# First layer of a hybrid decoder trunk: its weight splits on VectorE, its input normalised ahead of the projection, and a shorter build of the S5 power tables

## The chip, the cores and the metric

One core of one Trainium2 chip runs the whole kernel. The metric is device time in microseconds (us), the median of three runs. One further execution was profiled; rows of it are shown below.

## The reference

Two layers of a decoder trunk run on 512 tokens of width 1024, in float32. Each layer computes

```
h = RMSNorm(x) * g_pre
p = h @ W_in                      # columns shared out among 4 mixers
m = concat[GLA, DiffAttn, S5, RG-LRU](p) @ W_out
x = x + RMSNorm(m) * g_post
x = x + RMSNorm(sqrelu(RMSNorm(x) @ W1) @ W2)
```

The S5 mixer is a complex diagonal recurrence and needs tables of powers of its poles, for 128 steps, as cosine and sine parts.

## The kernel before

**Split products.** Each float32 product is made of three products of a faster format. A weight W is split into `wh` (a rounded copy) and `wl = W - wh`; an activation likewise into `h` and `l`. `w_part` does the split of one weight tile: `act.copy` on ScalarE writes `wh` (line 253), and a subtraction on VectorE or on GpSimd writes `wl` (line 254). `E.split_eng`, a string of `g` (GpSimd) and `v` (VectorE) that is cycled by the number of the tile, says which. In layer 1 it is `g` during the projection and the mixers, `gggv` for the output projection, `v` in the feed-forward part. In layer 2 the projection's weights come already split from DRAM (`early_gen` did it during layer 1's feed-forward part), the output projection's too, and the feed-forward part has `gggv`.

**Order.** Each engine runs its own instructions in the order that the scheduler wrote. SyncE issues all loads. Weights are loaded into three `raw` buffers and split into four `wh`/`wl` pairs ahead of their use (`w_get`, `w_split`, `w_load`); `home` can put a split weight into buffers of another pool.

**Layer 1's input.** The program loads `xT`, the input transposed by the host, in eight tiles. `hl` scales each by the gain column and splits it at once (lines 478 and 479). The norm isn't known yet: `SumSq` squares each tile on ScalarE (line 524), adds them up on VectorE (line 530), and TensorE sums over the partitions; VectorE then takes the reciprocal root, `rtok`, and TensorE spreads it to `rbc`, one value for each token. Every result of the projection is multiplied by it when it leaves PSUM (lines 1327, 1340, 1360 and 1374). The first projection, `dqk`, is done by `gemm_first`, which starts with the first tile that is there. 38 products of zeros run on TensorE first (`WARM`).

**Layer 2's input.** It is normalised first, in token-major tiles `X[b, c]`: ScalarE squares and sums (`accum_out`), `root` makes the reciprocal root of one block of 128 tokens (an activation with Sqrt and four VectorE operations), `dg` is the identity matrix times that root, and `make` multiplies X by `dg` on TensorE, which transposes and scales it (line 1298); the result leaves PSUM as `h` (ScalarE, line 1302) and `l` (VectorE, line 1303). `gemm_blocks` runs `dqk` over the first 256 tokens, calls `make(2)` for the others, then runs over these.

**Around them.** In layer 1 the order of the projections is dqk, dv, glr, gqk, gv, gog, u, rg, rx; the mixers' generators run in between (`advance`), and each starts when its inputs are there. `s5_prep_gen(0)` builds S5's tables during layer 1's mixers; `s5_prep_gen(1)` runs during layer 1's feed-forward part. Its powers are made by doubling: for e = 0 to 6, the first 2^e columns give the next 2^e through `cmul`, six VectorE operations (lines 671 to 676), separately for each half h of the states. `rope` reads q and k out of PSUM (line 1040). `diff_gen` runs the differential attention: row maxima (1072), `nb` (1073), exponentials on ScalarE, weights `cc` (1093).

Of the kernel before, what the change touches and what calls it, by code (L numbers as in the profile page):

```python
# [17 lines left out]
P = 128  # L18
# [94 lines left out]
def host_pack(I):  # L113
# [31 lines left out]
    return dict(xT=np.ascontiguousarray(I["x"][0].T), xt=np.ascontiguousarray(I["x"][0]),  # L145
# [25 lines left out]
def hybrid_trunk(ctx, tc, I, out, consts):  # L171
# [11 lines left out]
    def nm(s):  # L183
        uid[0] += 1
        return f"{s}_{uid[0]}"
# [144 lines left out]
    def gemm_first(wids, xs, consume):  # L330

        ps = [(pd if m // 2 % 2 else pg)() for m in range(4)]
        for kh in range(2):
            W = [w_get(w[kh]) for w in wids]

            def prod(m, k):
                cs = slice(m % 2 * P, m % 2 * P + P)
                Wm, kk = W[m // 2], 4 * kh + k
                mm3(ps[m], Wm[0][:, k, cs], Wm[1][:, k, cs], xs[kk][0], xs[kk][1], kk == 0, kk == 7)

            for k in range(2 if kh else 4):
                for m in range(4):
                    prod(m, k)
                yield
            if kh:
                for m in range(4):
                    for k in (2, 3):
                        prod(m, k)
                    with tc.high_priority(offset=O.evp):
                        consume(m, ps[m])  # L350
                    yield

# [159 lines left out]

    class SumSq:

        def __init__(self, eng, tail):
            self.acc, self.eng, self.tail = None, eng, tail
            self.ends = {}

        def add(self, c, src, hf=None):
            if hf is None:
                sq = wq("sq")
                act.activation(sq, src, AF.Square)
                if c >= self.tail:
                    self.ends[c] = sq
                elif self.acc is None:
                    self.acc = sq
                else:
                    self.eng.tensor_tensor(self.acc, self.acc, sq, ALU.add)  # L530
            else:
                if c not in self.ends:
                    self.ends[c] = wq("sq")
                act.activation(self.ends[c][:, 256 * hf:256 * hf + 256], src, AF.Square)

        def tok(self, bs=range(4)):
            ps = psm()
            tl = [self.acc] + list(self.ends.values())
            for b in bs:
                for i, t in enumerate(tl):  # L540
                    pe.matmul(ps[:, b:b + 1], t[:, b * P:b * P + P], C[:, C_BO + 6:C_BO + 7],
                              start=i == 0, stop=i == len(tl) - 1)
            return ps[:, bs[0]:bs[-1] + 1]

    def bcast_tok(col, n=4):
        ps = psm()
        for b in range(n):
            pe.matmul(ps[:, b * P:b * P + P], col[:, b:b + 1].to_broadcast([P, P]), ident,
                      start=True, stop=True)
        return ps[:, 0:n * P]  # L550
# [57 lines left out]
    def s5_prep_gen(l):  # L608
# [580 lines left out]
    sync.dma_start(PV, I["cols"])  # L1189
# [22 lines left out]
    setup_exp()  # L1212
# [28 lines left out]
    def post_norm(grow, g2=None):  # L1241
# [3 lines left out]
        ss, sx, part = small(8, "ss"), small(8, "sx"), small(4, "part")  # L1245
        gB = [wq("gB") for _ in range(2)]
        for c in range(2):
            sync.dma_start(gB[c], grow[:, c * 512:c * 512 + 512].to_broadcast([P, 512]))

            pool.tensor_scalar(gB[c], gB[c], 32.0, None, ALU.mult)  # L1250
        F, dg = {}, {}

        def stat(b, ct, o, f=None):
            act.activation(wq("sq"), o, AF.Square, accum_out=ss[:, 4 * ct + b:4 * ct + b + 1])
            F[b, ct] = o if f is None else f
            v.tensor_tensor(F[b, ct], o, gB[ct], ALU.mult)
            if ct == 0 and b == 3:
                v.tensor_scalar(part, ss[:, 0:4], D * EPS, None, ALU.add)

        def root(a, b):  # L1260

            y, t, xh = (small(1, k) for k in ("qy", "qt", "qh"))
            act.activation(t, a, AF.Sqrt, bias=b)
            v.tensor_scalar(xh, a, b, -0.5, ALU.add, ALU.mult)
            v.reciprocal(y, t)
            v.scalar_tensor_tensor(t, y, xh, y, ALU.mult, ALU.mult)
            v.scalar_tensor_tensor(y, t, 1.5, y, ALU.add, ALU.mult)
            return y

        def finish(b):  # L1270
            sc = root(ss[:, 4 + b:5 + b], part[:, b:b + 1])
            for c in range(2):
                if g2 is None:
                    o = wp.tile([P, 4, 256], F32, tag="raw", name=nm("o"), bufs=NRAW)
                    o = o.rearrange("p k c -> p (k c)")[:, 0:512]
                    v.scalar_tensor_tensor(o, F[b, c], sc, X[b, c], ALU.mult, ALU.add)
                    sync.dma_start(out[0, b * P:b * P + P, 512 * c:512 * c + 512], o)
                else:
                    v.scalar_tensor_tensor(X[b, c], F[b, c], sc, X[b, c], ALU.mult, ALU.add)
                    act.activation(wq("sq"), X[b, c], AF.Square, accum_out=sx[:, 2 * b + c:2 * b + c + 1])  # L1280
            if g2 is None:
                return
# [5 lines left out]
        def make(b):  # L1288
# [16 lines left out]
            for e in range(2):  # L1305
                for c in range(2):
                    spill(b + e, c)
# [3 lines left out]
    for l in range(NL):  # L1311

        O.__dict__.update(LAYER[l])
        if l == 0:
            E.split_eng = O.mix
        E.mix = {}
        st = {}

        rbc = None
        if l == 0:  # L1320
            rbc = cp.tile([P, T], F32, name="rbc")
            act.copy(rbc, bcast_tok(rtok))
        st["cosr"], st["sinr"] = wb("cosr"), wb("sinr")
        for k, c0 in (("cosr", C_COS), ("sinr", C_SIN)):
            sync.dma_start(st[k], consts[:, c0:c0 + T])
            if l == 0:
                v.tensor_tensor(st[k], st[k], rbc, ALU.mult)

        def ev_mul(key):
# [3 lines left out]
            def f(m, ps):  # L1333
                t = w(key)
                o, i, r = t, ps, rbc
                if key == "u":
                    o = t.rearrange("p (s t) -> p s t", s=4)
                    i, r = (x if x is None else x.rearrange("p (t s) -> p s t", s=4) for x in (ps, rbc))
                if l == 0:
                    v.tensor_tensor(o, i, r, ALU.mult)  # L1340
                else:
                    act.copy(o, i)
# [10 lines left out]
        def ev_silu(key):  # L1353
            st[key] = [None, None]

            def f(m, ps):
                t = wg(key)
                if l == 0:
                    v.tensor_tensor(t, ps, rbc, ALU.mult)
                act.activation(t, t if l == 0 else ps, AF.Silu)  # L1360
# [3 lines left out]
        def ev_tok(key):  # L1364
# [4 lines left out]
            def f(b, n, ps):  # L1369
                if l > 0:  # L1370
                    act.copy(tl[b // 2], ps)
                    return
# [185 lines left out]
```

## Time and profile before

| what | value |
|---|---|
| median of 3 runs | 1248.59 us (1243.89 to 1249.86) |
| the profiled execution's own time | 1246.94 us |
| its span, first to last instruction | 1244.9 us |
| TensorE busy | 1201.6 us (97%) |
| VectorE (DVE) busy | 683.9 us (55%) |
| ScalarE (ACT) busy | 509.2 us (41%) |
| GpSimd (POOL) busy | 194.2 us (16%) |
| mean granted TensorE clock | 0.976 |

Busy is time with at least one instruction under way; shares are averages over stages that differ. The chain is the work that ended last, followed back from the end, so that only what lies on it set the time. PE is TensorE, PEld its weight loads, DVE is VectorE, ACT ScalarE, POOL GpSimd, SP SyncE. The names with an arrow are output and input of an instruction, L is the line.

### The profile page before, as it was taken

The numbers are of one execution on the slowest core, as the hardware profiler recorded it, in microseconds if no ns is written. First come the engines' busy times: TensorE is split into PE (matmuls) and PEld (weight loads), VectorE is DVE, ScalarE is ACT, GpSimd is POOL, SyncE is SP. The second block draws the span as 40 slices with busy tenths as digits, with TensorE's granted clock in tenths as the row PEclk, the third lists the DMA queues.
The fourth block names the chain that finished last, engine by engine and source line by source line (L and its number), as shares of the span: only waits on it lengthen the run. The fifth ranks groups of instructions, "written<-read, shape, count | busy, mean of one in ns | idle before, by whom it ended". The sixth has DMA issues, their size and how long they took to land.

```text
span 1244.9 us, 17841 instructions
## 1 busy us (share of the span) xinstructions
PE 1201.6 (97%) x6684; PEld 967.6 (78%) x6684; DVE 683.9 (55%) x1605; ACT 509.2 (41%) x950; POOL 194.2 (16%) x148
## 2 busy tenths in 40 slices
PE   8988899899999999999999999999999999999997
PEld 6755566579888888888889776777988888888886
DVE  8987568578725576545474256575641131322335
ACT  5253622456735523424341356145542341332332
POOL 5321212300000001000000000010123323333330
PEclk9998889999999999999999999899999999999999
DMA  7343122456867887866754432355432333333221
GB/s 229 98 141 116 35 86 82 136 168 208 265 211 235 283 292 241 267 210 212 253 195 141 155 109 91 116 198 203 170 100 88 100 102 92 100 97 101 87 83 67
DMA packets 126037, 191.81 MB, mean 154 GB/s; under 512 B 10688, under 2 KB 65792, under 8 KB 125952
## 3 DMA queue, kind: packets, MB, share of 16 engines
q1 hardware_dynamic: 125952, 190.69, 47.4%
q8 instruction: 52, 0.85, 0.3%
q14 instruction: 33, 0.27, 0.1%
HBM read 146.35 MB, written 44.30 MB: 153 GB/s over the span
## 4 chain that ended last, share of the span: by engine, by line
PE 83%; DVE 10%; ACT 3%; DMA 1%; issue 1%; SPq 0%; DVEq 0%; ACTq 0%
PE pg L295 7%; PE pg L296 7%; PE pg L297 7%; PE pd L296 5%; PE pd L297 5%; PE pd L295 5%; PE pd L415 4%; PE pd L417 4%; PE pd L416 4%; PE pg L415 4%; PE pg L417 3%; PE pg L416 3%; PE pd L1063 2%; PE pm L415 2%; PE pm L416 2%; PE pm L417 2%
## 5 line engine op out<-in xcount | busy, mean ns | idle before, releaser
L253 ACT CAST wh<-raw 128x1024 fp32r<-128x1024 f32 (+1 forms) x160 | 157.4, 985 | 257.4 <-PE pg L416 88.2
L254 POOL TENSOR_TENSOR wl<-raw,wh 128x1024 fp32r<-128x1024 f32 (+1 forms) x69 | 156.9, 2275 | 383.3 <-ACT wh L253 380.7
L295 PE MATMUL pg<-h,wh 128*128 128x512 f32 (+1 forms) x496 | 189.4, 383 | 2.6 <-DVE glr L1392 2.5
L297 PE MATMUL pg<-h,wl 128*128 128x512 f32 (+1 forms) x496 | 188.9, 382 | 0.2 <-DVE wl L254 0.2
L296 PE MATMUL pg<-l,wh 128*128 128x512 f32 (+1 forms) x496 | 188.4, 381 | 0.5 <-DVE l L479 0.5
L254 DVE TENSOR_TENSOR wl<-raw,wh 128x1024 fp32r<-128x1024 f32 (+1 forms) x91 | 105.9, 1164 | 144.2 <-ACT wh L253 144.0
L297 PE MATMUL pd<-h,wl 128*128 128x512 f32 (+1 forms) x336 | 120.7, 360 | 0.0
L295 PE MATMUL pd<-h,wh 128*128 128x512 f32 (+1 forms) x336 | 120.6, 360 | 0.0
L296 PE MATMUL pd<-l,wh 128*128 128x512 f32 (+1 forms) x336 | 120.4, 359 | 0.0
L295 PEld LDWEIGHTS pg<-h,wh 128*128 128x128 f32 x496 | 95.7, 193 | 21.7 <-DVE glr L1392 2.9
L297 PEld LDWEIGHTS pg<-h,wl 128*128 128x128 f32 x496 | 95.7, 193 | 17.6 <-issue 1.4
L296 PEld LDWEIGHTS pg<-l,wh 128*128 128x128 f32 x496 | 95.8, 193 | 17.0 <-DVE l L479 1.2
L1474 DVE TENSOR_TENSOR s<-r 128x512 f32<-128x512 f32 x64 | 56.7, 886 | 87.4 <-ACT r L1473 87.4
L415 PE MATMUL pd<-wh,h 128*128 128x512 f32 x240 | 93.7, 390 | 0.9 <-DMA wh<-early 0.9
L417 PE MATMUL pd<-wl,h 128*128 128x512 f32 x240 | 93.6, 390 | 0.4 <-DVE wl L254 0.4
L416 PE MATMUL pd<-wh,l 128*128 128x512 f32 x240 | 93.4, 389 | 0.0
L415 PE MATMUL pg<-wh,h 128*128 128x512 f32 x208 | 81.4, 391 | 1.4 <-ACT h L475 1.4
L416 PE MATMUL pg<-wh,l 128*128 128x512 f32 x208 | 81.0, 389 | 0.0
L417 PE MATMUL pg<-wl,h 128*128 128x512 f32 x208 | 81.0, 389 | 0.0
L297 PEld LDWEIGHTS pd<-h,wl 128*128 128x128 f32 x336 | 63.6, 189 | 9.4
L295 PEld LDWEIGHTS pd<-h,wh 128*128 128x128 f32 x336 | 63.2, 189 | 9.6 <-ACT wh L253 0.3
L296 PEld LDWEIGHTS pd<-l,wh 128*128 128x128 f32 x336 | 63.5, 189 | 9.4
(421 smaller groups left out, 2162.6 us busy)
## 6 DMA issues: line engine op xcount, KB each, us to landing
raw<-in_ffn_w SPq DMA_DIRECT2D x128, 512.0 KB, 3.9
early<-eh SPq DMA_DIRECT2D x52, 256.0 KB, 3.1
early<-el SPq DMA_DIRECT2D x52, 256.0 KB, 4.1
wh<-early SPq DMA_DIRECT2D x23, 512.0 KB, 3.6
wl<-early SPq DMA_DIRECT2D x23, 512.0 KB, 4.7
ex<-in_w_in SPq DMA_DIRECT2D x36, 256.0 KB, 4.8
raw<-in_w_in SPq DMA_DIRECT2D x14, 512.0 KB, 3.7
xd<-xr SPq DMA_DIRECT2D x24, 256.0 KB, 2.9
```

The lines of the kernel that those rows point to most:

```text
L253: act.copy(h[:, k], raws[i][:, k])
L254: eng.tensor_tensor(lo[:, k], raws[i][:, k], h[:, k].bitcast(F32), ALU.subtract)
L295: pe.matmul(ps, wh, xh, start=first, stop=False, **kw)
L296: pe.matmul(ps, wh, xl, start=False, stop=False, **kw)
L297: pe.matmul(ps, wl, xh, start=False, stop=last, **kw)
L415: pe.matmul(o, xs[kk][0][:, ts_], h, start=kk == 0, stop=False)
L416: pe.matmul(o, xs[kk][1][:, ts_], h, start=False, stop=False)
L417: pe.matmul(o, xs[kk][0][:, ts_], lo, start=False, stop=kk == 7)
L1063: pe.matmul(pp[c], qs[h // 2][r:r + 32, i * P:i * P + P], ks[h // 2][r:r + 32, 0:pp[c].shape[1]], start=i == blocks[0], stop=False, tile_p ...
L1474: v.tensor_tensor(s, r, r, ALU.mult)
```

## The change

- **Splits.** All splits of layer 1 go to VectorE: `mix` and `out` become `v`. Layer 2 keeps `gggv`. The first three weights go to buffers of other pools through `home`.
- **Input.** `xT`, `SumSq`, `bcast_tok`, `gemm_first`, `rtok` and `rbc` are gone. The part of `post_norm` that normalised layer 2's input becomes `pre_norm` (`half`, `done`, `make`), and layer 1 uses it too: token-major x is loaded in the order blocks 0, constants, 1, parameter columns, weights 0 and 1, blocks 2 and 3, weight 2; then `make(0)`, and `gemm_blocks` calls `make(2)`. Results leave PSUM by `act.copy` without a factor. `WARM` is 80.
- **S5.** The first 16 powers of both halves and both parts are made in one tile `pw`, with four VectorE operations for each of four doublings; two ScalarE copies for each half put them into the tables, and only e = 4 to 6 are done for each half.

```diff
+        pw = wq("pw")[:, 0:256].rearrange("p (c j m) -> p c j m", c=2, j=8)
+        pool.memset(pw[:, 0, :, 0:1], 1.0)
+        pool.memset(pw[:, 1, :, 0:1], 0.0)
+
+        def bc2(x, m):
+            return x.unsqueeze(1).unsqueeze(3).to_broadcast([P, 2, 8, m])
+
+        for e in range(4):
+            m = 1 << e
+            wr, wi = (w[:, 8 * e + 8:8 * e + 16] for w in (csw, snw))
+            xa, xb = (wq("cm")[:, 0:16 * m].rearrange("p (c j m) -> p c j m", c=2, j=8) for _ in range(2))
+            tt(xa, pw[:, :, :, 0:m], bc2(wr, m), ALU.mult)
+            tt(xb, pw[:, :, :, 0:m], bc2(wi, m), ALU.mult)
+            tt(pw[:, 0, :, m:2 * m], xa[:, 0], xb[:, 1], ALU.subtract)
+            tt(pw[:, 1, :, m:2 * m], xa[:, 1], xb[:, 0], ALU.add)
+            yield
         for h in range(2):
             js = slice(4 * h, 4 * h + 4)
             tabs = [wt(k) for k in ("COS", "SIN", "RC")]
             ct, st, rc = (t.rearrange("p (j c) -> p j c", j=4) for t in tabs)
-            pool.memset(ct[:, :, 0:1], 1.0)
-            pool.memset(st[:, :, 0:1], 0.0)
-            for e in range(7):
+            for c, t in enumerate((ct, st)):
+                act.copy(t[:, :, 0:16], pw[:, c, js])
+            for e in range(4, 7):
                 m = 1 << e
                 wr, wi = (w[:, 8 * e + 8:8 * e + 16] for w in (csw, snw))
-                cmul(ct[:, :, m:2 * m], st[:, :, m:2 * m], ct[:, :, 0:m], st[:, :, 0:m],
-                     bc(wr, m, js), bc(wi, m, js), 4, m)
+                a_r, a_i = (pw[:, c, js] for c in range(2)) if e == 4 else (ct[:, :, 0:m], st[:, :, 0:m])
+                cmul(ct[:, :, m:2 * m], st[:, :, m:2 * m], a_r, a_i, bc(wr, m, js), bc(wi, m, js), 4, m)
                 yield
...
-    ssq = SumSq(v, 7)
-    xin = []
-    for c in range(8):
-        w2 = (c // 4 * 2, c // 4 * 2 + 1)
-        if c % 4 == 0:
-            for i in w2:
-                w_raw(i)
-                w_open(i)
-        xin.append(wl("x"))
-        sync.dma_start(xin[c], I["xT"][c * P:c * P + P, :])
-        for i in w2:
-            sync.dma_start(raws[i][:, c % 4], specs[i][:, c % 4])
-        XG[c] = hl(xin[c], pv("ln_mix_pre", 0, 8, c))
-        for i, e in zip(w2, (v, pool)):
-            w_part(i, slice(c % 4, c % 4 + 1), e)
-        if c % 4 == 3:
-            for i in w2:
-                del raws[i]
-    pos[:] = [4, 4]
-    sync.dma_start(C, consts[:, 0:C_N])
-    w_load(3 + NRAW)
-    for c in range(8):
-        ssq.add(c, xin[c])
-    ms = small(4, "ms4")
-    v.tensor_scalar(ms, ssq.tok(), 1.0 / D, EPS, ALU.mult, ALU.add)
-    rtok = small(4, "rkeep")
-    v.tensor_copy(rtok, rsqrt(ms, 4))
...
+    def pre_norm(g2, keep):
+        sx, dg = small(8, "sx"), {}
+        def half(b, c):
+            act.activation(wq("sq"), X[b, c], AF.Square, accum_out=sx[:, 2 * b + c:2 * b + c + 1])
+        def done(b):
...
+    E.split_eng = "v"
+    half, done, make = pre_norm(lambda c: pv("ln_mix_pre", 0, 8, c), False)
+    x_load(0)
+    sync.dma_start(C, consts[:, 0:C_N])
+    x_load(1)
+    sync.dma_start(PV, I["cols"])
+    home.update(enumerate((wg, wg, wb)))
+    w_load(1)
+    x_load(2)
+    x_load(3)
+    w_load(2)
+    for b in range(4):
+        for c in range(2):
+            half(b, c)
+        done(b)
+        if b == 1:
+            make(0)
+            setup_exp()
...
-            rbc = cp.tile([P, T], F32, name="rbc")
-            act.copy(rbc, bcast_tok(rtok))
...
-                if l == 0:
-                    v.tensor_tensor(o, i, r, ALU.mult)
-                else:
-                    act.copy(o, i)
+                    o, i = t.rearrange("p (s t) -> p s t", s=4), ps.rearrange("p (t s) -> p s t", s=4)
...
-                g = gemm_first if l == 0 else lambda *a: gemm_blocks(*a, make)
-                g = g(WID[l, "dqk"], XG, lambda m, ps: evs[m // 2](m % 2, ps))
+                g = gemm_blocks(WID[l, "dqk"], XG, lambda m, ps: evs[m // 2](m % 2, ps), make)
...
-WARM = 38
+WARM = 80
...
-         mix='g', out='gggv', ff='v', m_outer=False, on_pool=(), pin=False, wt_act=False, add=(), prep_at=1),
+         mix='v', out='v', ff='v', m_outer=False, on_pool=(), pin=False, wt_act=False, add=(), prep_at=1),
```

## Rows read from the trace of the kernel before

**Rows 1.** The page: the chain that ended last, by engine.

```profile
PE 83%; DVE 10%; ACT 3%; DMA 1%; issue 1%; SPq 0%; DVEq 0%; ACTq 0%
```

**Rows 2.** Windows: us, busy (count) by engine, clock, DMA share, GB/s.

```profile
0.00:10.00 10.00, 8.97 (x58) 7.12 (x58) 6.49 (x28) 7.05 (x15) 4.32 (x10) 1.00 0.79 243
0.00:52.00 52.00, 47.26 (x274) 38.80 (x274) 48.49 (x174) 24.66 (x46) 25.05 (x26) 0.97 0.58 177
52.00:117.00 65.00, 52.36 (x332) 37.77 (x331) 58.71 (x272) 28.09 (x85) 15.04 (x19) 0.90 0.43 138
117.00:227.00 110.00, 100.76 (x794) 69.33 (x793) 71.76 (x166) 42.35 (x77) 23.92 (x20) 0.89 0.24 72
643.00:700.00 57.00, 57.00 (x421) 53.20 (x420) 24.02 (x59) 13.54 (x34) 1.10 (x3) 1.00 0.55 191
700.00:846.00 146.00, 143.73 (x1063) 102.17 (x1061) 85.49 (x230) 69.17 (x165) 7.37 (x13) 0.96 0.39 134
```

**Rows 3.** The chain over 0 to 282 us: start, us, what.

```profile
25.07 2.24 DVE sf L585
...
125.55 2.56 DVE nb L1073
...
228.59 2.77 DVE xc L861
```

**Rows 4.** Single lines, 0 to 282 us: count, ns min/median/max.

```profile
L585 DVE SCALAR_TENSOR_TENSOR sf<-sf,sf x7: 149/155/2330, 23.8 to 27.4; 128x4 f32<-128x4 f32 x7
...
L1073 DVE TENSOR_SCALAR nb<-mx x16: 150/160/2548, 62.6 to 159.6; 128x2 f32<-128x2 f32 x16
...
L861 DVE SCALAR_TENSOR_TENSOR xc<-rx,PV,xc x6: 726/739/2853, 228.5 to 237.6; 128x511 f32<-128x511 f32 x2, 128x510 f32<-128x510 f32 x2, 128x509 f32<-128x509 f32 x2
```

**Rows 5.** GpSimd in order of time, 0 to 320 us.

```profile
125.20 2.40 POOL L254 TENSOR_TENSOR wl<-raw,wh 128x1024 fp32r<-128x1024 f32 x1 [18.54 <-ACT wh L253]
```

**Rows 6.** Line 254, the splits, 0 to 282 us, and its waits.

```profile
L254 POOL TENSOR_TENSOR wl<-raw,wh x27: 740/2382/4332, 6.2 to 245.0; 128x1024 fp32r<-128x1024 f32 x19, 128x256 fp32r<-128x256 f32 x8
L254 DVEq EVENT_SEMAPHORE  x12: 21/21/1309, 5.3 to 278.9; - x12
L254 DVE TENSOR_TENSOR wl<-raw,wh x12: 407/680/1226, 5.4 to 280.5; 128x256 fp32r<-128x256 f32 x8, 128x1024 fp32r<-128x1024 f32 x4
...
  ACT wh L253: 127.5, 24
```

**Rows 7.** Line 1340: the projection's results times the reciprocal norm.

```profile
L1340 DVE TENSOR_TENSOR gqk<-pg,rbc x2: 675/680/684, 72.6 to 81.8; 128x512 f32<-128x512 f32 x2
L1340 DVE TENSOR_TENSOR u<-pg,rbc x2: 1093/1105/1117, 160.4 to 163.9; 128x512 f32<-128x512 f32 x2
```

**Rows 8.** Line 673 by form, 80 to 111 us: busy us, mean ns.

```profile
L673 DVE TENSOR_TENSOR COS<-cm,cm 128x128 f32<-128x128 f32 x2 | 0.6, 286 | 0.0
...
L673 DVE TENSOR_TENSOR COS<-cm,cm 128x4 f32<-128x4 f32 x2 | 0.3, 155 | 0.0
```

**Rows 9.** The first product of each layer, in order of time.

```profile
5.11 0.74 PE L295 MATMUL pg<-h,wh 128*128 128x512 f32 x2
...
647.82 0.28 PE L295 MATMUL pd<-h,wh 128*128 128x256 f32 x1
```

**Rows 10.** Rope's last reads of the first projection, both layers.

```profile
L1040 DVE STREAM_SHUFFLE sh<-pd x2: 759/760/762, 36.5 to 37.8; 128x512 f32<-128x512 f32 x2
...
L1040 DVE STREAM_SHUFFLE sh<-pg x2: 737/739/741, 671.7 to 674.6; 128x512 f32<-128x512 f32 x2
```

**Rows 11.** Normalisation: its products on TensorE, and layer 2's evictions.

```profile
L1298 PE MATMUL pg<-dg,xr x16: 270/275/377, 282.2 to 285.3; 128*128 128x128 f32 x16
...
L1298 PE MATMUL pg<-dg,xr x32: 270/275/275, 642.9 to 880.8; 128*128 128x128 f32 x32
...
L1302 ACT ACTIVATE h<-pm,PV x8: 466/470/474, 647.7 to 659.7; 128x256 fp32r<-128x256 f32 x8
...
L1303 DVE SCALAR_TENSOR_TENSOR l<-pm,PV,h x8: 472/476/485, 648.2 to 660.2; 128x256 fp32r<-128x256 f32 x8
```

More of the change, by code (lines that the diff above doesn't have):

```diff
@@ L144, in host_pack @@
         tab[l, :, K_GLR:K_GLR + P] = I["w_in"][l, :, 512:528].reshape(8, P, 16).transpose(1, 0, 2).reshape(P, P)
-    return dict(xT=np.ascontiguousarray(I["x"][0].T), xt=np.ascontiguousarray(I["x"][0]),
+    return dict(xt=np.ascontiguousarray(I["x"][0]),
                 mpost=np.ascontiguousarray(I["ln_mix_post"]), cols=cols, tab=tab)
@@ L328, in gemm_T @@
                     yield
[L330 to L351, printed above, removed]
     def gemm_blocks(wids, xs, consume, need):
@@ L511, in rsqrt @@
         return y
[L513 to L528, printed above, removed]
-                else:
[L530 to L550, printed above, removed]
     cmask = cp.tile([P, P], BF16, name="cmask")
@@ L1231, in hybrid_trunk @@
-    pos[:] = [4, 4]
-    sync.dma_start(C, consts[:, 0:C_N])
-    w_load(3 + NRAW)
-    for c in range(8):
-        ssq.add(c, xin[c])
-    ms = small(4, "ms4")
-    v.tensor_scalar(ms, ssq.tok(), 1.0 / D, EPS, ALU.mult, ALU.add)
-    rtok = small(4, "rkeep")
-    v.tensor_copy(rtok, rsqrt(ms, 4))
[L1241 to L1282, printed above, removed]
@@ new lines, in root @@
+    def root(a, b):
+        y, t, xh = (small(1, k) for k in ("qy", "qt", "qh"))
+        act.activation(t, a, AF.Sqrt, bias=b)
+        v.tensor_scalar(xh, a, b, -0.5, ALU.add, ALU.mult)
+        v.reciprocal(y, t)
+        v.scalar_tensor_tensor(t, y, xh, y, ALU.mult, ALU.mult)
+        v.scalar_tensor_tensor(y, t, 1.5, y, ALU.add, ALU.mult)
+        return y
+    def pre_norm(g2, keep):
[3 more added lines that the diff above has]
+        def done(b):
@@ L1304, in make, with x_load @@
                                            ALU.mult, ALU.subtract)
-            for e in range(2):
-                for c in range(2):
-                    spill(b + e, c)
+            if keep:
+                for e in range(2):
+                    for c in range(2):
+                        spill(b + e, c)
+        return half, done, make
+    def x_load(b):
+        for c in range(2):
+            X[b, c] = wl("x")
+            sync.dma_start(X[b, c], XD[b, c])
+    E.split_eng = "v"
+    half, done, make = pre_norm(lambda c: pv("ln_mix_pre", 0, 8, c), False)
@@ new lines, in hybrid_trunk, with post_norm, stat, finish @@
+    x_load(0)
[8 more added lines that the diff above has]
+    for b in range(4):
+        for c in range(2):
+            half(b, c)
[3 more added lines that the diff above has]
+            setup_exp()
+    def post_norm(grow, g2=None):
+        ss, part = small(8, "ss"), small(4, "part")
+        half, done, make = pre_norm(g2, True) if g2 is not None else (None, None, None)
+        gB = [wq("gB") for _ in range(2)]
+        for c in range(2):
+            sync.dma_start(gB[c], grow[:, c * 512:c * 512 + 512].to_broadcast([P, 512]))
+            pool.tensor_scalar(gB[c], gB[c], 32.0, None, ALU.mult)
+        F = {}
+        def stat(b, ct, o, f=None):
+            act.activation(wq("sq"), o, AF.Square, accum_out=ss[:, 4 * ct + b:4 * ct + b + 1])
+            F[b, ct] = o if f is None else f
+            v.tensor_tensor(F[b, ct], o, gB[ct], ALU.mult)
+            if ct == 0 and b == 3:
+                v.tensor_scalar(part, ss[:, 0:4], D * EPS, None, ALU.add)
+        def finish(b):
+            sc = root(ss[:, 4 + b:5 + b], part[:, b:b + 1])
+            for c in range(2):
+                if g2 is None:
+                    o = wp.tile([P, 4, 256], F32, tag="raw", name=nm("o"), bufs=NRAW)
+                    o = o.rearrange("p k c -> p (k c)")[:, 0:512]
+                    v.scalar_tensor_tensor(o, F[b, c], sc, X[b, c], ALU.mult, ALU.add)
+                    sync.dma_start(out[0, b * P:b * P + P, 512 * c:512 * c + 512], o)
+                else:
+                    v.scalar_tensor_tensor(X[b, c], F[b, c], sc, X[b, c], ALU.mult, ALU.add)
+                    half(b, c)
+            if g2 is not None:
+                done(b)
@@ L1334, in f @@
                 t = w(key)
[L1335 removed]
+                o, i = t, ps
                 if key == "u":
[L1337 to L1342 removed]
+                    o, i = t.rearrange("p (s t) -> p s t", s=4), ps.rearrange("p (t s) -> p s t", s=4)
+                act.copy(o, i)
                 st[key][m] = t
@@ L1369, in f @@
             def f(b, n, ps):
-                if l > 0:
-                    act.copy(tl[b // 2], ps)
-                    return
-                for i in range(n):
-                    act.activation(st[key][b + i], ps[:, 256 * i:256 * i + 256], AF.Copy,
-                                   scale=rtok[:, b + i:b + i + 1])
+                act.copy(tl[b // 2], ps)
             return f
@@ L1390, in glr_gen @@
             t = wg("glr")[0:32]
-            if l == 0:
-                v.tensor_tensor(t, ps, rbc[0:32], ALU.mult)
-            else:
-                v.tensor_copy(t, ps)
+            v.tensor_copy(t, ps)
             st["glr"] = t
```

11 lines of the change are left out of this document (1 added, 10 removed).

## The prediction

> **What bounds the kernel now.** I read the page's chain first. TensorE holds most of it and VectorE 10% [rows 1], which is at most 124 us of the 1244.9 us span. Then I cut the span into stages with the windows. Layer 1's projection and mixers, up to the normalisation behind the output projection (TensorE's products for it begin at 282.2 us [rows 11]), fill 0 to 282 us. Up to 117 us VectorE is busy 107 of 117 us while TensorE has gaps and runs below its full 2.4 GHz level for part of the time (granted clock 0.90); from 117 to 227 us the clock is 0.89 and neither engine is full [rows 2]. Layer 2 does the same projection and mixers, without weight splits and without building tables: TensorE is busy 57.0 of 57 and 143.7 of 146 us, at 1.00 and 0.96, with VectorE at about half [rows 2]. So the stage that the change touches is late by VectorE, and nearly all of VectorE's 124 us must lie there: they are 0.44 of these 282 us.
>
> The chain in order of time shows what VectorE does there. Between 25 and 229 us it holds 13 pieces of VectorE work of 1.67 to 2.77 us, 29.55 us in all, of which the first, one from the middle and the last are shown [rows 3]. They are no large operations: line 1073 works on two columns and takes 160 ns in the median, but 2548 ns once; line 585 takes 155 ns and once 2330; line 861 739 and once 2853 [rows 4]. GpSimd's row gives the reason: a split runs on GpSimd from 125.20 us for 2.40 us, and the slow line 1073 starts at 125.55 and ends as that split ends [rows 5, 3]. The 27 splits on GpSimd [rows 6] thus stop VectorE, small operation or not.
>
> The Trainium skill says so too: "SBUF — State Buffer", section "SBUF: two separate sides", describes a port pair shared by VectorE and GpSimd that whichever starts first keeps for its whole instruction. The trace agrees, by the 2548 ns beside the 160.
>
> **The change, part by part.** *Stalls.* Without splits on GpSimd the 13 pieces shrink to their ordinary lengths. Those are some 0.16 us for eight, 0.2 to 0.3 for four and 0.74 for line 861 [rows 4, 8], 3.0 us together, so 26.5 us leave the chain. What is late next is TensorE or ScalarE, which were only covered by the stall, so the gain lies between 0 and 26.5. I take two thirds, 17.7, as layer 2 shows TensorE running nearly through where VectorE isn't late [rows 2].
>
> *Splits on VectorE.* 19 whole splits and 8 quarters move from GpSimd. VectorE's whole ones take at most 1.23 us, quarters from 0.41 [rows 6]. At 1.2 us: 19 x 1.2 = 22.8; the first four weights, whole or in two halves, 4.8 in place of some 4 us for 8 quarters on VectorE. Together +23.6 us of VectorE.
>
> *Multiplications by the reciprocal norm.* Ten of 0.68 us go (gqk, rg, rx, gog, and the two rope tables, counted like gqk), two for u of 1.1 and one for glr, counted 0.6: 9.6 us; the six additions of squares, of the same shape, 6 x 0.68 = 4.1; the reciprocal root, some 14 tiny operations, 2.2 [rows 7, 4]. In their place come four roots with `dg`, 4 x 5 tiny operations at 0.16 and 4 x 0.28 (like a form of 128 columns), 4.3 us, and 16 evictions of `l` at 0.476 us for 8 of 512 columns, some +1.5 [rows 4, 8, 11]. ScalarE takes over the copies and sums its squares while squaring them, eight as before; I cost this at nothing, since it is busy 28 of 65 and 42 of 110 us [rows 2]. Without that room the eight or so copies at 0.6 us would be 5 us.
>
> *S5's powers.* Forty-eight operations go (4 to 32 columns), at some 0.17 us each, 8.2 us; 16 with 16 to 128 columns come, at some 0.21, 3.4 (0.155 is measured at 4 columns, 0.286 at 128 [rows 8]): -4.8 us. The four ScalarE copies hide as above. In layer 1's feed-forward part the same saving is hidden by TensorE and worth nothing.
>
> VectorE's own work so changes by 23.6 - 9.6 - 4.1 - 2.2 + 4.3 + 1.5 - 4.8 = +8.7 us. At its share of the chain, 0.44, that costs 3.8 us (0 if it fills gaps, 8.7 if all lies on the path).
>
> *The start.* Before, TensorE's first product is at 5.11 us [rows 9] and `rope` reads the last piece of dqk at 37.8 [rows 10]. Now nothing starts before blocks 0 and 1 of x are there, squared, rooted, transposed and evicted. Bytes: 1.05 MB of x, 0.22 of constants, 0.09 of columns, 1.05 of weights 0 and 1, 2.4 MB; at 243 GB/s [rows 2] 9.9 us, and some 2 us until the first lands: 12; with a cast and a subtraction the first product is at about 13 us. Layer 2's `gemm_blocks` goes from 647.8 to `rope`'s last read at 674.6 [rows 9, 10], 27 us with `make(2)` inside. So dqk ends near 40 us, 2 to 3 us later, and 6 later if weight 3, which waits for one of three raw buffers, is late for the second half. SyncE has fewer loads to issue than before, the two tables of rope need no factor any more, and the longer warm-up ends before the first product, so these cost nothing; without the wait for x the warm-up would be in the way. I take +3 (0 to +6).
>
> *The clock.* From 52 to 227 us it stood at 0.90 and 0.89; layer 2's like stretch has 0.96 [rows 2]. Reaching that would give 65 x 0.06 + 110 x 0.07 = 11.6 us; an estimate of half, 5.8, since VectorE stays fuller than in layer 2.
>
> Sum: -17.7 + 3.8 + 3 - 5.8 = -16.7 us. The profiled execution took 1246.94 us, so 1230.2; the median of the runs is 1.65 above it, so 1232 us. The stages after 282 us stay: TensorE sets them, and layer 2's splits still go to GpSimd.
>
> **The rivals.** *The pace of layer 2* (chance 0.18). If VectorE is never late any more, dqk starts at 13 us and takes what layer 2's part takes: from 647.8 us to the end of the same products, 880.8 [rows 9, 11], 233 us, and an estimate of 4 for the tables' products, so the stage ends near 250 in place of 282 us: -32, 1217 us. For it: GpSimd no longer interferes. Against: VectorE still does splits and tables that layer 2 hasn't.
>
> *TensorE takes the place* (0.14). The stalls were largely covered: half of 26.5 comes off, the clock gives nothing, the start costs 6: -13.2 + 3.8 + 6 = -3.4, 1245 us.
>
> *VectorE waits for the casts* (0.08). A split needs ScalarE's cast, which needs a free buffer. GpSimd stood waiting for casts for 127.5 us in 24 waits; VectorE's longest wait at a split was 1.3 us [rows 6]. Now what stands behind a split on VectorE, above all the row maxima that ScalarE's exponentials wait for, waits with it. At 1.3 us for each of 19 splits it is +24.7: -16.7 + 24.7 = +8, 1257 us. It decides from 0.9 us a split. Against it: the median wait is 21 ns [rows 6].
>
> *A full VectorE* (0.04). Before 117 us VectorE has 10 us to spare [rows 2]. If the stalls return in another form and all its added work counts, +8.7 + 3 = +12: 1260 us. The Trainium skill speaks for this side: "Perfetto Trace Analysis", section "Optimizing Scalar/DVE Operations", advises moving work off a saturated VectorE, even to GpSimd, though it adds that the shared port may undo it; by its first half this change goes the wrong way. The trace sides with the second: 2.4 us of stall against 1.2 us of split.
>
> **How the numbers follow.** The forecast has a chance of 0.56; with the rivals that is 1. 0.5% (6.2 us) is about what a measurement of this kernel can tell from no change. Faster: the forecast and layer 2's pace, 0.74; the same, 0.14; slower, 0.12. The low end takes all of the stalls and the clock and no cost: -26.5 - 11.6 = -38, 1211 us. The high end is set between the third and the fourth case, 1252, with the slower cases mostly outside.
>
> **What would show it.** In the changed profile: no split on GpSimd before 282 us; the maxima of lines 585, 1073 and 861 near their medians; VectorE's share of the chain well below 10%; the clock from 52 to 227 us above 0.90; a first product at about 13 us, and dqk done near 40; the first normalisation of the feed-forward part near 265 us instead of 282. The prediction fails if casts come late and VectorE stands before its splits, or if the start is later than 46 us at the end of dqk.

## The result: 39 us faster, over twice the forecast

The changed kernel takes 1207.0 us (median of 4 runs, 1204.12 to 1210.65); the kernel before took 1246.24 beside it. The ratio is 0.9701, 95% interval 0.9663 to 0.9738. The forecast was 1232 us, 16.7 us faster, with a range down to 1211. The direction was right; the size forecast was less than half of what came, and the time lies below the range.

The page's chain, by engine: VectorE's share fell from 10% [rows 1] to 7%.

```profile
PE 86%; DVE 7%; ACT 3%; DMA 2%; issue 1%; DVEq 0%; SPq 0%; ACTq 0%
```

The windows of the changed kernel, with the columns of [rows 2]; the last one is the whole of layer 1's projection and mixers, up to the products of the normalisation behind them (line 1201 in this kernel).

```profile
0.00:52.00 52.00, 50.01 (x440) 48.81 (x441) 43.65 (x203) 26.52 (x55) 3.40 (x12) 1.00 0.54 176
52.00:117.00 65.00, 63.22 (x394) 47.19 (x393) 52.39 (x224) 40.92 (x95) 6.08 (x16) 0.97 0.50 155
117.00:227.00 110.00, 106.57 (x867) 76.02 (x866) 85.45 (x206) 55.93 (x113) 5.95 (x11) 1.00 0.33 103
0.00:243.70 243.70, 236.50 (x1771) 185.58 (x1772) 194.43 (x669) 133.35 (x289) 16.13 (x41) 0.99 0.45 143
```

Where [rows 2] had TensorE busy 52.36 of 65 us at a clock of 0.90 and 100.76 of 110 at 0.89, it is now busy 63.22 at 0.97 and 106.57 at 1.00 (1.00 is the level of 2.4 GHz, and a mean below it has a part at 1.2): the gaps and the lower clock went together. Single lines: the normalisation's products behind the mixers, `nb` (line 1028 here), the convolution's line 861 (816 here) and the splits.

```profile
L1201 PE MATMUL pg<-dg,xr x16: 270/275/377, 243.7 to 245.7; 128*128 128x128 f32 x16
...
L1028 DVE TENSOR_SCALAR nb<-mx x16: 149/159/170, 57.4 to 146.9; 128x2 f32<-128x2 f32 x16
...
L816 DVE SCALAR_TENSOR_TENSOR xc<-rx,PV,xc x6: 723/742/1082, 194.7 to 201.1; 128x511 f32<-128x511 f32 x2, 128x510 f32<-128x510 f32 x2, 128x509 f32<-128x509 f32 x2
...
L254 DVEq EVENT_SEMAPHORE  x28: 21/50/1381, 19.3 to 280.8; - x28
L254 DVE TENSOR_TENSOR wl<-raw,wh x28: 1201/1222/1227, 19.5 to 281.4; 128x1024 fp32r<-128x1024 f32 x28
...
  ACT wh L253: 3.7, 8
```

The stage ends at 243.7 us in place of 282.2 [rows 11]; near 265 was forecast. `nb`, at up to 2548 ns before [rows 4], takes at most 170 ns, line 816 at most 1082 where line 861 took up to 2853. Up to 282 us VectorE now does 28 whole splits of 1.22 us and waits for their casts 3.7 us in all, where GpSimd had waited 127.5 [rows 6].

For the account of the stage, the kernel before over its own length:

```profile
0.00:282.20 282.20, 250.74 (x1593) 183.02 (x1594) 218.39 (x675) 128.16 (x267) 73.23 (x70) 0.92 0.39 122
```

TensorE had 282.2 - 250.7 = 31.5 us of gaps; now it has 243.7 - 236.5 = 7.2. Its busy time at a mean clock of 0.92 is 230.7 us at full speed, so 20.0 us went into the lower clock; now 236.5 at 0.99 leaves 2.4. So 24.3 us came from gaps and an estimated 17.7 from the clock, and some 3.4 us of further work (longer warm-up, products with `dg`) went the other way: 38.6, the 38.5 us by which the stage is shorter. The sum has to come out, since the further work is what is left over. The clock column has two decimals and is a mean over the whole stage, gaps included, so the clock's term and the further work are good to some 3 us only; the gaps don't depend on it. Behind 243.7 us the rest is as long as before: 1205.9 - 243.7 = 962.2 beside 1244.9 - 282.2 = 962.7 us. Layer 2 and the feed-forward parts gave nothing.

The start: first product, last read by `rope`.

```profile
12.05 0.36 PE L295 MATMUL pd<-h,wh 128*128 128x256 f32 x1
...
L995 DVE STREAM_SHUFFLE sh<-pg x2: 737/744/750, 36.4 to 39.3; 128x512 f32<-128x512 f32 x2
```

12.05 and 39.3 us, beside 13 and near 40 forecast and 37.8 before [rows 10].

### The profile page after: what moved, and what is told of

Read it like the earlier page. It is cut to its first block, busy times and chain, and to the rows that moved or that the text cites. A ratio compares the mean times of both kernels' runs of the same rounds, so it can differ in the third digit from the quotient of the medians.

```text
span 1205.9 us, 18120 instructions
## 1 busy us (share of the span) xinstructions
PE 1184.1 (98%) x6862; PEld 967.8 (80%) x6862; DVE 655.8 (54%) x1560; ACT 513.3 (43%) x972; POOL 137.4 (11%) x117
## 4 chain that ended last, share of the span: by engine, by line
PE 86%; DVE 7%; ACT 3%; DMA 2%; issue 1%; DVEq 0%; SPq 0%; ACTq 0%
PE pg L295 8%; PE pg L297 8%; PE pg L296 7%; PE pd L295 5%; PE pd L297 5%; PE pd L296 5%; PE pd L392 4%; PE pd L394 4%; PE pd L393 4%; PE pg L392 4%; PE pg L393 4%; PE pg L394 4%; PE pd L1018 2%; PE pm L392 2%; PE pm L393 2%; PE pm L394 2%
## 5 line engine op out<-in xcount | busy, mean ns | idle before, releaser
L253 ACT CAST wh<-raw 128x1024 fp32r<-128x1024 f32 x145 | 152.1, 1050 | 246.4 <-PE pg L393 82.1
L254 DVE TENSOR_TENSOR wl<-raw,wh 128x1024 fp32r<-128x1024 f32 x103 | 126.0, 1224 | 146.9 <-ACT wh L253 139.8
L254 POOL TENSOR_TENSOR wl<-raw,wh 128x1024 fp32r<-128x1024 f32 x42 | 100.4, 2391 | 258.1 <-ACT wh L253 258.1
L296 PE MATMUL pd<-l,wh 128*128 128x512 f32 (+1 forms) x352 | 123.5, 351 | 0.3 <-DVE l L1206 0.3
L295 PE MATMUL pd<-h,wh 128*128 128x512 f32 (+1 forms) x352 | 123.8, 352 | 0.0
L297 PE MATMUL pd<-h,wl 128*128 128x512 f32 (+1 forms) x352 | 123.4, 351 | 0.0
L296 PEld LDWEIGHTS pd<-l,wh 128*128 128x128 f32 x352 | 66.6, 189 | 9.3 <-DVE l L1206 0.6
L297 PEld LDWEIGHTS pd<-h,wl 128*128 128x128 f32 x352 | 66.6, 189 | 8.8
L295 PEld LDWEIGHTS pd<-h,wh 128*128 128x128 f32 x352 | 66.6, 189 | 8.7
```

What stands on the lines that cost most here:

```text
L253: act.copy(h[:, k], raws[i][:, k])
L254: eng.tensor_tensor(lo[:, k], raws[i][:, k], h[:, k].bitcast(F32), ALU.subtract)
L295: pe.matmul(ps, wh, xh, start=first, stop=False, **kw)
L296: pe.matmul(ps, wh, xl, start=False, stop=False, **kw)
L297: pe.matmul(ps, wl, xh, start=False, stop=last, **kw)
```

## The experiments

All were timed against the kernel before on the same chip; the ratios are to it. "The changed kernel" is 0.9701 by the same measure. The chip was not the same for all experiments, so differences to the changed kernel are safer by the ratios (times 1246 us) than by the medians. Stage means layer 1's projection and mixers as above.

### One part alone, one part undone

**Only the splits.** In the kernel before:

```diff
-        for i, e in zip(w2, (v, pool)):
+        for i, e in zip(w2, (v, v)):
-         mix='g', out='gggv', ff='v'
+         mix='v', out='v', ff='v'
```

> The kernel before with one edit: layer 1's splits all on VectorE. Theory A (splits on GpSimd stop VectorE, TensorE then has gaps and its clock falls; the three come off together): 25 to 35 us faster than before, the granted clock from 52 to 227 us at 0.97 or more, no small VectorE operation over 1 us before 282 us. Theory B (the new input and its longer warm-up close the early gaps and take VectorE's multiplications away, the splits are a minor part): at most 12 us faster, the clock from 52 to 227 us still near 0.90.

1224.05 us, ratio 0.9844 (0.9814 to 0.9875): 21 us of the 39, between the theories. Its windows, the last one its whole stage:

```profile
52.00:117.00 65.00, 62.49 (x413) 46.67 (x411) 57.97 (x265) 38.14 (x92) 5.88 (x17) 1.00 0.50 152
117.00:227.00 110.00, 103.74 (x838) 73.54 (x838) 81.74 (x201) 52.23 (x96) 7.00 (x12) 0.97 0.29 93
0.00:254.50 254.50, 236.11 (x1592) 179.24 (x1593) 206.02 (x712) 129.47 (x271) 17.64 (x43) 0.96 0.44 138
```

Gaps 254.5 - 236.1 = 18.4 us in place of 31.5, clock 0.96 (9.4 us in place of 20.0). No `nb` takes more than 0.32 us any more. So the clock and the small operations are as theory A had them, the time is under its range, and theory A holds for the larger part: the stage is 27.7 us shorter, though VectorE does all the splits and still all the multiplications. The run as a whole gains less than its stage: layer 2's stage took 239 us here and 236 before.

**All but the splits.** In the changed kernel:

```diff
-    E.split_eng = "v"
+    E.split_eng = "vg"
-         mix='v', out='v', ff='v'
+         mix='g', out='gggv', ff='v'
```

> The changed kernel with layer 1's splits back on GpSimd where they were (the first four taken in turn by VectorE and GpSimd). Theory A: most of the gain is gone, 25 us or more slower than the changed kernel, small VectorE operations of over 2 us are back, the clock from 52 to 227 us under 0.95. Theory B: at most 15 us slower than the changed kernel.

1244.36 us, ratio 0.9988 (0.996 to 1.0016): with the splits on GpSimd the other parts together are worth nothing, as theory A says. Its window from 60 to 100 us, where the kernel before had TensorE busy 33.7 us at 0.92, and its `nb`:

```profile
60.00:100.00 40.00, 28.94 (x191) 21.23 (x191) 34.78 (x153) 20.82 (x55) 12.00 (x14) 0.78 0.56 183
```

```profile
L1028 DVE TENSOR_SCALAR nb<-mx x16: 150/166/2800, 69.3 to 151.9; 128x2 f32<-128x2 f32 x16
```

VectorE is busy 34.8 of 40 us, TensorE has 11 us of gaps and a clock of 0.78, and an `nb` takes 2.8 us again.

**S5's powers as before.** The loop over e = 0 to 6 for each half in place of `pw`, in the changed kernel.

> The changed kernel with S5's powers made as before, for each half from the first. By the prediction's term 4.8 us more VectorE work in layer 1, on the path at 0.44: about 2 us slower, 0 to 5. If VectorE's early load is what holds the clock down: 8 us or more slower.

1207.41 us, ratio 0.9714 (0.968 to 0.9749): no difference to the changed kernel. Where VectorE is no longer late, this part is worth nothing that can be measured.

**A shorter warm-up.** `WARM = 38` in the changed kernel.

> The changed kernel with 38 warm-up products in place of 80. Theory A: within 2 us of the changed kernel, as TensorE only waits for x there. If the clock's state at the first products matters (theory B): a clock under 1.00 from 8 to 30 us and 4 to 10 us slower.

1212.81 us (1206.33 to 1214.05), ratio 0.9743 (0.9705 to 0.9782); the interval overlaps that of the changed kernel. Windows of the start, this run first, then the changed kernel:

```profile
0.00:10.00 10.00, 6.25 (x48) 5.78 (x49) 3.42 (x25) 6.74 (x14) 2.88 (x11) 0.90 0.80 257
10.00:30.00 20.00, 19.47 (x158) 19.05 (x157) 15.15 (x47) 14.67 (x34) 0.53 (x1) 0.96 0.75 246
30.00:60.00 30.00, 29.26 (x216) 26.55 (x217) 28.24 (x148) 5.18 (x8) 0.53 (x1) 0.94 0.27 74
```

```profile
0.00:10.00 10.00, 8.01 (x93) 7.65 (x94) 3.44 (x25) 7.09 (x15) 2.87 (x11) 1.00 0.77 252
10.00:30.00 20.00, 20.00 (x172) 19.89 (x171) 18.46 (x54) 15.50 (x36) 0.53 (x1) 1.00 0.89 292
30.00:60.00 30.00, 30.00 (x221) 26.25 (x220) 29.75 (x167) 6.53 (x11) 0.52 (x1) 1.00 0.22 62
```

With the gap ahead of the first products the clock is 0.90, 0.96 and 0.94 in place of 1.00, as theory B had it. Its stage ends at 246.6 us, 2.9 later; the rest of the profiled difference is in layer 2. So the long warm-up, which bridges the wait for x, keeps the clock up; that this is worth about 3 us rests on one profile of each, and the times don't separate it from nothing. I had costed it at nothing.

**The input alone, and S5 alone.** In the kernel before: the whole new input with splits and S5 as they were; and `pw` alone.

> The kernel before with the new input alone (and its warm-up): splits on GpSimd as before, S5's powers as before. After the first runs two readings are left. Theory A (VectorE, full and stalled up to about 110 us, sets the stage whatever TensorE does at the start): the same as before within 5 us, a gap of TensorE between 60 and 100 us with a clock near 0.8. Theory C (the input is worth 17 us by itself and only the new S5 build together with GpSimd's splits took it back): 10 us or more faster.

> The kernel before with S5's powers built in the new way alone. VectorE's load up to 110 us falls by some 5 us at a share of the path that is high there: 2 to 5 us faster by theory A. If operations of that size are covered by others: no change within 2 us.

1236.71 us, ratio 0.9922 (0.9887 to 0.9957), and 1237.1, ratio 0.9902 (0.9867 to 0.9936). Each is some 10 us faster alone (12 by the ratio for S5), and both together are worth nothing (all but the splits, above). Both expectations missed: the first is on the edge between its readings, the second beyond its own. With GpSimd's splits in place a small change of order moves the moments at which they stop VectorE; that this is why the two don't add is argued, not shown.

### GpSimd's reading, by itself

In the changed kernel, at each of 23 splits, extra work on GpSimd that nobody needs, a ghost:

```diff
         act.copy(h[:, k], raws[i][:, k])
+        if i < 26:
+            ghost(raws[i], h)
...
+    def ghost(x, h):
+        for e in range(2):
+            pool.tensor_tensor(gsc, x[:, 2 * e:2 * e + 2].rearrange("p k c -> p (k c)"),
+                               h[:, 2 * e:2 * e + 2].rearrange("p k c -> p (k c)").bitcast(F32), ALU.subtract)
```

> The changed kernel, and beside each of 23 splits of layer 1 on VectorE two subtractions on GpSimd of 512 columns each, into a buffer that nobody reads; VectorE's work stays as it is. A raw weight buffer is held until GpSimd is done with it. Theory A (GpSimd's reading stops VectorE): 15 to 40 us slower than the changed kernel, VectorE operations stretched by 1 to 2 us, gaps and a lower clock on TensorE. Rival (it was the distribution of the work, the stretched operations being covered): within 5 us of the changed kernel.

1258.59 us, ratio 1.0082 (1.0054 to 1.011): 47 us slower than the changed kernel by the ratios, 52 by the medians, above the range expected and slower than the kernel before too. But here GpSimd also holds the raw buffers. Without that, reading the cast weight and a constant tile:

```diff
+            pool.tensor_tensor(gsc, hv, gone, ALU.subtract)
```

> The changed kernel, and beside each of 23 splits of layer 1 two subtractions on GpSimd of 512 columns each that read the cast weight and a constant tile; the raw weight buffers are not held. Theory A (GpSimd's reading stops VectorE and the gaps lower the clock): 20 to 45 us slower than the changed kernel, near the kernel before. Rival (the first ghost run was slow because raw buffers were held and weights came late): within 8 us of the changed kernel.

1255.39 us, ratio 1.0058 (1.0027 to 1.009), 44 us slower than the changed kernel by the ratios and 48 by the medians, at the upper end of the range expected. The rival is out. With GpSimd about as long at work, but nearly all of it writing:

```diff
+            pool.tensor_tensor(gsc[:, 0:4], hv[:, 0:4], gone[:, 0:4], ALU.subtract)
+            for _ in range(2):
+                pool.memset(gsc, 0.0)
```

> As the run before it, with the GpSimd work changed: a subtraction of 4 columns and two memsets of 512 columns in place of each subtraction of 512 columns, so that GpSimd is about as long at work but hardly reads. If reading is what stops VectorE: within 4 us of the changed kernel. If any GpSimd instruction stops it: 15 us or more slower.

1210.71 us, ratio 0.9687 (0.9645 to 0.9728): no difference to the changed kernel. The two side by side, by the window from 60 to 180 us and the whole stage; reading first, writing second:

```profile
60.00:180.00 120.00, 101.36 (x669) 73.02 (x668) 96.03 (x338) 60.96 (x150) 35.02 (x34) 0.91 0.34 106
0.00:286.00 286.00, 249.83 (x1770) 192.80 (x1771) 232.84 (x672) 134.82 (x289) 96.12 (x88) 0.95 0.39 122
```

```profile
60.00:180.00 120.00, 114.43 (x935) 83.10 (x934) 94.07 (x334) 67.62 (x162) 41.57 (x84) 0.99 0.39 119
0.00:246.20 246.20, 236.54 (x1770) 185.42 (x1771) 196.26 (x670) 133.76 (x289) 92.56 (x180) 0.99 0.45 142
```

GpSimd is busy 96.12 us in the one and 92.56 in the other. With reading, TensorE has 36.2 us of gaps, with writing 9.7. VectorE does as many operations in either, 672 and 670, but takes 232.84 us for them beside GpSimd's reading and 196.26 beside its writing (194.43 in the changed kernel). This is the clearest pair of the study: not GpSimd's being busy, but its subtractions of two tiles beside VectorE's work cost the time. Whether a GpSimd operation that reads one tile does the same was not tested. How it looks in order of time with reading, GpSimd first, then VectorE:

```profile
106.85 7.40 POOL L252 TENSOR_TENSOR gsc<-wh,gone 128x512 f32<-128x512 f32 x4 [2.33 <-ACT wh L262]
```

```profile
107.94 1.53 DVE L623 TENSOR_TENSOR cm<-COS,cies 128x256 f32<-128x256 f32 x1
109.40 2.33 DVE L265 TENSOR_TENSOR wl<-raw,wh 128x1024 fp32r<-128x1024 f32 x1
111.65 1.48 DVE L624 TENSOR_TENSOR cm<-SIN,cs 128x256 f32<-128x256 f32 x1
113.05 1.22 DVE L1039 TENSOR_SCALAR nb<-mx 128x2 f32<-128x2 f32 x1
```

While GpSimd subtracts from 106.85 us for 7.4 us, a VectorE split takes 2.33 us where its like takes 1.22, and `nb` on two columns takes 1.22 us.

### The price of VectorE's own work

**Multiplications back.** In the changed kernel, layer 1's results and rope tables are multiplied on VectorE by a tile of ones, `rbc` (gog, glr and the two tables by like lines):

```diff
-                act.copy(o, i)
+                if l == 0:
+                    r = rbc.rearrange("p (t s) -> p s t", s=4) if key == "u" else rbc
+                    v.tensor_tensor(o, i, r, ALU.mult)
+                else:
+                    act.copy(o, i)
```

> The changed kernel, with the results of layer 1's projection and the two rope tables multiplied on VectorE by a tile of ones, as the kernel before multiplied them by the reciprocal norm: the 9 us of VectorE work are back, the rest stays. If VectorE's added work sets what the new input gained beside the splits (17 us): 10 to 17 us slower than the changed kernel. If that gain came from TensorE's full start and its clock: 0 to 4 us slower, as 9.6 us at 0.44 of the path.

1215.89 us, ratio 0.9743 (0.9697 to 0.9789), 5 us slower than the changed kernel by the ratios, 9 by the medians; its stage ends at 251.6 us, 7.9 later. The expectation's first reading was too high, the second too low: of this work, some 9 us between a product's end and its first reader, more than 0.44 seems to lie on the path. The intervals of the two kernels overlap, so that is not shown.

**Splits doubled.** At each of 23 splits two more subtractions of 512 columns on VectorE, into a buffer that nobody reads:

```diff
+            v.tensor_tensor(gsc, hv, gone, ALU.subtract)
```

> The changed kernel, and beside each of 23 splits of layer 1 two subtractions of 512 columns on VectorE into a buffer that nobody reads: 46 operations of some 0.6 to 0.7 us, 28 to 32 us more VectorE work. By the prediction's price (0.44 of the path): 12 to 14 us slower. If VectorE's work at these places is wholly on the path, as the multiplications nearly were: 25 us or more. If it fills gaps: under 5 us.

1224.64 us (1213.33 to 1228.38), ratio 0.9786 (0.9727 to 0.9845).

```profile
L252 DVE TENSOR_TENSOR gsc<-wh,gone x46: 666/684/694, 19.3 to 247.4; 128x512 f32<-128x512 f32 x46
```

46 x 0.684 = 31.5 us of added work cost 10.6 us by the ratios (0.0085 x 1246) and 17.6 by the medians, 0.34 to 0.56 of it. The prediction's price of 0.44 lies inside; the interval is too wide to say more.

### Is the clock a loss of its own?

Ten products of zeros ahead of each of 16 groups of transposes in layer 1's attention, in either kernel:

```diff
             pt = pd()
+            if l == 0:
+                for _ in range(10):
+                    pe.matmul(pt[:, 0:P], z, z, start=True, stop=True)
```

> The kernel before, with 160 products of zeros on TensorE in layer 1's attention: 10 ahead of each of 16 groups of transposes, where TensorE waits for VectorE's weights. If the low clock from 60 to 180 us is a loss of its own that activity takes away, beside the gaps: the clock there at 0.95 or more and 5 to 15 us faster than before. If the clock only follows the gaps and the stalls set the pace: the clock rises, and the time stays within 4 us of before or gets longer by a part of the 17 us that the products take.

> The changed kernel with the same 160 products. The clock is at 1.00 already and TensorE has hardly a gap there, so by both readings the products only cost: 8 to 18 us slower than the changed kernel (160 at 0.108 us are 17 us). It prices the filling that the run beside it pays where it doesn't fall into gaps.

The kernel before takes 1255.02 us with them, ratio 1.0067 (1.0036 to 1.0097); the changed kernel 1223.67, ratio 0.9813 (0.9785 to 0.9842). Windows of the kernel before without and with the filling:

```profile
60.00:180.00 120.00, 103.89 (x617) 70.62 (x616) 87.16 (x321) 57.41 (x144) 26.40 (x27) 0.85 0.29 93
180.00:227.00 47.00, 43.71 (x483) 32.78 (x480) 35.31 (x68) 12.74 (x17) 11.24 (x10) 1.00 0.35 101
52.00:227.00 175.00, 153.12 (x1124) 107.10 (x1124) 130.47 (x438) 70.45 (x162) 38.96 (x39) 0.89 0.31 97
```

```profile
60.00:180.00 120.00, 106.31 (x783) 75.95 (x783) 88.40 (x337) 58.10 (x145) 25.93 (x27) 0.92 0.29 93
180.00:227.00 47.00, 44.08 (x352) 33.96 (x351) 29.03 (x48) 9.07 (x12) 7.79 (x10) 0.76 0.22 66
52.00:227.00 175.00, 158.18 (x1171) 114.22 (x1169) 125.43 (x422) 68.35 (x161) 37.77 (x40) 0.88 0.28 88
```

The clock from 60 to 180 us rises from 0.85 to 0.92, and the time doesn't fall; behind, from 180 to 227 us, it drops from 1.00 to 0.76. Over 52 to 227 us it stays where it was, 0.88 beside 0.89: the low stretches moved and did not go. In the changed kernel the products cost 14 us by the ratios and 16.7 by the medians, most of their 17; in the kernel before 8 to 10, so some 6 or 7 of the 17 us fell into gaps. Such filling doesn't give the 20 us. What the kernel before would take with its gaps and a clock of 1.00 throughout, this run can't say, since the clock over the stage didn't rise; whether the clock is a loss of its own stays open.

### Another order

`"u"` moved ahead of `"gqk"` in layer 1's order, in the changed kernel.

> The changed kernel with layer 1's projection of u moved ahead of gqk, so that S5's long chain of VectorE work starts earlier and the end of the stage, from 200 to 244 us, where TensorE waits for ScalarE, VectorE and loads, gets shorter. If that tail is S5's: 3 to 10 us faster than the changed kernel. If it is the last mixer's (rx): the same within 2 us, or slower as GLA now starts later.

1240.05 us, ratio 0.9939 (0.9916 to 0.9961): 30 us slower than the changed kernel by the ratios, 33 by the medians, far outside either reading. Between 52 and 117 us, in an execution of 1247.22 us, the longest of its ten:

```profile
52.00:117.00 65.00, 55.26 (x297) 34.66 (x297) 55.74 (x237) 30.01 (x90) 4.80 (x14) 0.79 0.50 155
```

TensorE has 9.7 us of gaps there and a clock of 0.79: fewer gaps than the kernel before, which had 12.6, and a lower clock than its 0.90 [rows 2], with no split on GpSimd. So an order that doesn't fit costs more than the splits alone did; why, wasn't followed up. No version here is clearly faster than the changed kernel.

## Why the prediction fell short

**The stalls: right cause, little over half the size.** The prediction took two thirds of 26.5 us, arguing that other work would come late next, and 3.8 us off for VectorE's added work: 13.9 us net of gaps. The stage lost 24.3 us of gaps, all else included. The cut to two thirds is a step that failed: with all of the stalls, 26.5 - 3.8 = 22.7 us, the term would have fitted. "TensorE or ScalarE, which were only covered by the stall" hardly came late: the splits alone took 13.1 us of gaps away with all of their own cost paid, and the changed kernel has 7.2 us left. That GpSimd's subtractions stretch VectorE's work and bring the gaps is shown by the pair of ghost runs, and that the splits did it in the kernel before by the run with only the splits changed.

**The clock: the term that failed most.** "An estimate of half, 5.8" stands beside some 17.7 us measured. I had split one effect in two: a price for the stalls and a separate, halved one for the clock, with layer 2's 0.96 as the most that could come. Moving the splits alone took 13.1 us of gaps and some 10.6 us of the clock's loss away, and in the ghost pair GpSimd's work alone moves both, so here they came and went together. They don't go in a fixed proportion: 17.7 / 24.3 = 0.7 us of clock for each us of gap from the kernel before to the changed one, but 0.4 in the ghost pair (26.5 us of gaps, 0.95 beside 0.99) and about 2 with the splits doubled on VectorE, where TensorE has 12.1 us of gaps in place of 7.2 and some 12 us of clock loss in place of 2.4:

```profile
0.00:260.10 260.10, 248.02 (x1770) 192.78 (x1771) 217.99 (x707) 133.19 (x285) 17.49 (x42) 0.95 0.42 132
```

The bound was too low as well: the stage now stands at 0.99. With the stalls whole and the clock as measured, the prediction's own sum would be -26.5 + 3.8 + 3 - 17.7 = -37.4 us, beside 38.5 for the stage: the mechanism was right, these two sizes were not. That the low end, -38, came near was luck: it joined a clock of at most 11.6 to no cost at all.

**A reading that was not exact.** The slow `nb` did not end with the split, at 127.60 us, but at 125.55 + 2.56 = 128.11, with a memset that GpSimd did next:

```profile
127.55 0.53 POOL L951 MEMSET rst<- 128x512 f32 x1
```

**VectorE's work.** +23.6 us of splits at 0.44 of the path agrees with the doubled splits (0.34 to 0.56). The multiplications that go were priced alike and seem worth a little more, 5 to 9 us in place of 4.2. S5's powers were worth nothing in the end, in place of 2.

**The start.** +3 us forecast; the first product and the end of dqk came at 12.05 and 39.3 us, as worked out. That the warm-up costs nothing was true, but without its added length the stage would be some 3 us longer by the one profile, since it bridges TensorE's wait for x.

**The rivals.** "The pace of layer 2" was the case that came nearest: 233 us from the first product were forecast for it, 243.7 - 12.05 = 231.6 were measured. The 233 ran to the last of the normalisation's 16 products; to the first, as here, layer 2 took 879.2 - 647.8 = 231.4:

```profile
L1298 PE MATMUL pg<-dg,xr x16: 270/275/275, 879.2 to 880.8; 128*128 128x128 f32 x16
```

That the two agree to 0.2 us is partly chance, as layer 1 has products for tables that layer 2 lacks. The rival's own time, 1217 us, is 10 above the measured one: 4 us of it for those tables, the rest its later start and end, the rounding of the stage and a kernel before that ran 2.4 us faster beside this one. What spoke for it, TensorE's 143.7 of 146 us in layer 2, was the better guide than the list of stalls; I gave it 0.18 because VectorE still has splits and tables, which left TensorE only 7.2 us of gaps. VectorE waiting for casts came to 3.7 us, so that rival is out, and so is a full VectorE: up to 117 us it has 117 - 43.65 - 52.39 = 21 us to spare, in the stage 49.3 (243.7 - 194.4). The advice that spoke for that case, the Trainium skill's "Perfetto Trace Analysis", section "Optimizing Scalar/DVE Operations", did not hold here: the splits alone, brought back from GpSimd, made the kernel 21 us faster; its warning of the shared port does hold.

**What stays open.** Why the new input and the new S5 build are worth 10 us each but nothing together while GpSimd does the splits. What makes up the 17 us between the splits alone and the changed kernel: the stage is 10.8 us shorter (254.5 to 243.7), which the multiplications (7.9) and the warm-up (2.9) would account for by single profiles, but the loading by tokens, the squares and the buffers of `home` weren't undone one by one. Whether the clock is a loss beside the gaps. And how far the few us by which layer 2's stage differs between runs (232 to 239 us, with the same program there) are the clock.

## What to carry to other kernels

Before moving a subtraction to GpSimd to relieve VectorE, look in the trace for VectorE operations of a few columns that last as long as GpSimd's: here 2.4 us of GpSimd work stopped VectorE for as long and cost more than the 1.2 us that VectorE needs for the same split, while as much GpSimd work that nearly only wrote cost no time that could be measured. Price such a stall together with the loss of TensorE's clock that comes with its gaps, and take that loss from runs, as its size per us of gap varied here from 0.4 to 2. Where another layer of the same kernel does the same work without the disturbance, give its pace more weight than a list of stalls; in this one case it was the better guide.

## What the runs showed of the hardware

Memsets on GpSimd of like length cost the kernel no time that could be measured: 92.56 us of busy GpSimd, mostly writing, left the stage at 246.2 us, 96.12 us with the reading made it 286. They did stop VectorE now and then: in the run with the memsets one `nb` took 1.48 us in place of 0.16 and ended with two memsets of the kernel's own.

```profile
L1041 DVE TENSOR_SCALAR nb<-mx x16: 150/160/1476, 58.1 to 149.3; 128x2 f32<-128x2 f32 x16
...
124.27 1.48 DVE L1041 TENSOR_SCALAR nb<-mx 128x2 f32<-128x2 f32 x1
...
124.74 0.98 POOL L972 MEMSET am<- 128x512 f32 x2
```

The Trainium skill, "SBUF — State Buffer", section "SBUF: two separate sides", names two kinds of VectorE operation that contend with GpSimd: those in a two-port mode, and those with two SBUF inputs, the latter only against GpSimd operations that read. The trace agrees for splits, which have two inputs: 2.33 us beside GpSimd's subtractions, at most 1.23 in the changed kernel. `nb`, which has one input, was stopped by reading (2548 ns [rows 4]) and by memsets; whether it runs in a two-port mode no run here shows.

The granted clock fell where TensorE had gaps, but the gaps of a stretch don't fix it: 0.78 where TensorE was busy 28.94 of 40 us and 1.00 where it had no gap, yet from 180 to 227 us 1.00 with 43.71 of 47 us busy in the kernel before and 0.76 with 44.08 busy in the same kernel with the filling. After the wait for x behind the shorter warm-up the mean was still 0.94 between 30 and 60 us.
